# Storing the split weights of the projections in DRAM once and loading the parts again for the later token blocks

## The chip, the cores and the metric

One core of a Trainium2 chip runs the whole kernel. Five engines work side by side, each through its own list of instructions in a fixed order: TensorE (PE, matmuls; its weight loads are shown as PEld), VectorE (DVE), ScalarE (ACT), GpSimd (POOL) and SyncE (SP, which here issues every DMA). An engine waits for another by a semaphore, and what stands behind a waiting instruction in its list waits too. The metric is the time of one execution in microseconds (us) on the device; three runs of the kernel before gave 2217.27, 2220.72 and 2221.74 us, so the median is 2220.72 us.

## The reference, cut to what matters

The input is 2048 tokens of width 1024, float32. One layer is computed.

```python
h = rmsnorm(x, norm_mix)
proj = h @ w_in                      # 1024 x 2832
a_q, a_f, a_i, a_g, b_x, b_g, c_q, c_k, c_v, c_g, c_lr = split(proj)
o_a = hgrn2_mixer(a_q, a_f, a_i, a_g, ...)      # chunked gated linear attention, 4 heads
o_b = rglru_mixer(b_x, b_g, ...)                # causal conv, gates, linear recurrence over tokens
o_c = gla_mixer(c_q, c_k, c_v, c_g, c_lr, ...)  # chunked gated linear attention, 4 heads
x = x + concatenate([o_a, o_b, o_c]) @ w_out    # 1024 x 1024
h = rmsnorm(x, norm_ffn)
gate = causal_dwconv(h @ ffn_w_gate)            # 1024 x 2688
x = x + (gelu(gate) * (h @ ffn_w_val)) @ ffn_w_down
out = rmsnorm(x, norm_final)
```

The change touches only the weights `w_in` and `w_out`.

## The kernel before, in words

**Matmuls in three products.** A float32 operand is split into two parts of type fp32r: the high part is a rounded copy, the low part is what the copy lost (`split`, L110: a copy on one engine, then a subtraction on another). A product is three matmuls, high by high, high by low, low by high (`mm3`, L134).

**Weights.** `load_w` (L115) fetches one piece of a weight matrix, at most 128 partitions by 1024 elements, into a buffer `wr` (pool `wraw`, 3 buffers), and splits it into `wh` and `wl` (pool `wsp`, 3 buffers each). A buffer of `wh`/`wl` is taken again when the matmuls that read it have ended. `W_SPLIT` (L38) says by a tag which engines do the copy and the subtraction, and how far ahead in the priorities the split is put: "z" and "qk" both on DVE, "cv", "ai", "g", "bg" and "out" copy on ACT and subtract on DVE, "bi" copies on DVE and subtracts on POOL.

**Token blocks.** The 2048 tokens are done in four blocks of 512. A block's normed and transposed input `hT` is kept as two parts and, for the first three blocks, stored to DRAM (`h_d`) for a second use.

**First half, groups A and C (L229 to L712).** For every block, `in_steps` projects: two pieces for the forget gates ("z"), three pieces of 272 columns for the values of C ("cv"), four for queries and keys ("qk"), two pieces of 256 columns for the values of A ("ai") and four for the output gates ("g"): 15 calls of `load_w` in a block. `mix_steps` is the chunked attention, many short steps that go from DVE to PE and back. `run_steps` merges the projections of block b+1 with the mixing of block b. In the last block `s_bg` also makes group B's eight projections for that block ("bg") and stores them to DRAM.

**Second half, group B and the output projection (L715 to L875).** `b_in` makes group B's eight projections for the first three blocks ("bi"), reading `hT` again from DRAM, `b_mix` the gates and the recurrence, `b_fin` the split of the concatenated outputs into `oh` and `ol`, and `b_out` the output projection. `b_out` goes through four groups of 256 columns; for each it calls `load_w` twice (rows 0 to 511 and 512 to 1023) and then runs four tiles of 128 tokens, 24 matmuls of 256 columns each, twelve on the first piece and twelve on the second. For every tile a piece of x (`xr`, 4 buffers) is loaded by SP, DVE adds the product to it (L834), and SP stores it to `x2_d`. `b_out` of block b-1 stands behind `b_in` and `b_mix` of block b in the program.

**Third part.** The gated MLP with its own weights, from about 968 us on, until the end.

**Order.** The tile framework lays each engine's list by a priority, which is the place in the program, moved forward where `tc.high_priority` says so, and by when it reckons an instruction can start. `b_in` of block 0 is moved forward to the mixing of the last block. The order on the chip is then fixed.

Of the kernel before, what the change touches and what calls it, by code (L numbers as in the profile page):

```python
# [8 lines left out]
F32 = mybir.dt.float32  # L9
F32R = mybir.dt.float32r  # L10
# [6 lines left out]
P = 128  # L17
D = 1024
KT = D // P
# [14 lines left out]
A_Q, A_F, A_I, A_G, B_X, B_G, C_Q, C_K, C_V, C_G, C_LR = (  # L34
    0, 256, 512, 768, 1024, 1536, 2048, 2176, 2304, 2560, 2816)
# [9 lines left out]
def kernel(ctx: ExitStack, tc: tile.TileContext, x, norm_mix, w_in, hgrn_lower_bounds, hgrn_norm,  # L45
# [4 lines left out]
    vec, act, pool, pe, sync = nc.vector, nc.scalar, nc.gpsimd, nc.tensor, nc.sync  # L50
    x, out, w_in, w_out = x[0], out[0], w_in[0], w_out[0]
# [4 lines left out]
    def pool_at(stack, nbytes, name, bufs, **kw):  # L56

        stack.enter_context(tc.tile_pool(name="pad_" + name, bufs=1, **kw)).tile([P, nbytes // 4], F32, name="pad")
        return stack.enter_context(tc.tile_pool(name=name, bufs=bufs, **kw))
# [3 lines left out]
    wsp = pool_at(ctx, 320, "wsp", 3)  # L63
# [5 lines left out]
    dram = ctx.enter_context(tc.tile_pool(name="dram", bufs=1, space=DRAM))  # L69
# [16 lines left out]
    def mm_bank():  # L86
        return bank("mm", 4)
# [4 lines left out]
    def sc_bank():  # L92
        return bank("sc", 2)
# [10 lines left out]
    def copy(eng, o, i):  # L104
        if eng is act:
            act.activation(o, i, AF.Copy)  # L106
        else:
            eng.tensor_copy(o, i)

    def split(raw, hi, lo, e_hi=act, e_lo=vec):  # L110

        copy(e_hi, hi, raw)
        e_lo.tensor_tensor(lo, raw, hi.bitcast(F32), op=ALU.subtract)  # L113

    def load_w(src, n1, n2, tag, tail=None, wpool=None, wcols=D):  # L115

        def part(pool_, dt, nm):
            return pool_.tile([P, wcols], dt, name=nm, tag=nm)[:, :n1 * n2].rearrange("p (a b) -> p a b", b=n2)
        hl = [part(wpool or wsp, F32R, "wh"), part(wpool or wsp, F32R, "wl")]
        raw = part(wraw, F32, "wr")  # L120
        if tail is None:
            sync.dma_start(out=raw, in_=src)
        else:
            m = src.shape[-1]
            sync.dma_start(out=raw[:, :, :m], in_=src)
            sync.dma_start(out=raw[:, :, m:], in_=tail)
        e_hi, e_lo, ahead = W_SPLIT[tag]
        with tc.high_priority(offset=ahead):
            split(raw, hl[0], hl[1], getattr(nc, e_hi), getattr(nc, e_lo))
        return hl  # L130

    w_in_v = w_in.rearrange("(kt p) c -> p kt c", p=P)
# [46 lines left out]
    def proj_mm(w, hT):  # L179
        o = mm_bank()  # L180
        for kt in range(KT):
            mm3(o, [a[:, kt, :] for a in w], [a[:, kt, :] for a in hT], kt == 0, kt == KT - 1)
        return o

    def proj(hT, col, tag):

        return proj_mm(load_w(w_in_v[:, :, col:col + P], KT, P, tag), hT)

    def merged(a, b):

# [38 lines left out]
    with ExitStack() as cx:  # L229
# [13 lines left out]
        def in_steps(b, B):  # L243
# [13 lines left out]
            def s_vw(col, n):  # L257
                if n > 256:
                    B["V"] = blk.tile([P, NTK, 528], F32, name="V")
                B["kn"] = 3 if n > 256 else 4  # L260
                B["ws"] = []
                for k0 in range(0, KT, B["kn"]):
                    ks = slice(k0, min(k0 + B["kn"], KT))
                    B["ws"].append(load_w(w_in_v[:, ks, col:col + 256], ks.stop - k0, n, "cv" if n > 256 else "ai",
                                          w_in_v[:, ks, C_LR:C_LR + 16] if n > 256 else None))

            def s_v(n, at, t):
                o = mm_bank()
# [42 lines left out]
            for t in range(NTK):  # L311
                steps.append(lambda t=t: (s_vw(C_V, 272) if t == 0 and b > 0 else None, s_v(272, 256, t)))
# [245 lines left out]
        for gi, group in enumerate((rows, frows)):  # L558
            n = sum(r[2] for r in group)
# [7 lines left out]
            cols = const.tile([P, n], F32, name=f"pcol{gi}")  # L567
# [78 lines left out]
        for b in LEVELS[:5]:  # L646
            n = 64 // b
# [67 lines left out]
    with ExitStack() as cy:  # L715
# [3 lines left out]
        with ExitStack() as cx:  # L719
# [12 lines left out]
            w_out_v = w_out.rearrange("(kt p) c -> p kt c", p=P)  # L732
# [87 lines left out]
            def b_out(b, B):  # L820
                oh = B["oh"]
                for qd in range(4):
                    cols = slice(256 * qd, 256 * qd + 256)
                    ws = [load_w(w_out_v[:, k0:k0 + 4, cols], 4, 256, "out") for k0 in (0, 4)]
                    for t in range(NTK):
                        rw = slice(t * P, (t + 1) * P)
                        xr = xrp.tile([P, 256], F32, name="xr")
                        sync.dma_start(out=xr, in_=x[b * TB + t * P:b * TB + (t + 1) * P, cols])
                        o = sc_bank()
                        for kt in range(KT):  # L830
                            mm3(o[:, :256], [a[:, kt, t * P:(t + 1) * P] for a in oh],
                                [a[:, kt % 4, :] for a in ws[kt // 4]], kt == 0, kt == KT - 1)
                        with tc.high_priority(offset=320):
                            vec.tensor_tensor(xr, o[:, :256], xr, op=ALU.add)  # L834
                        sync.dma_start(out=x2_d[b][rw, cols], in_=xr)
# [479 lines left out]
```

## Time and profile before

| what | value |
|---|---|
| median of three runs | 2220.72 us |
| the profiled execution's own time | 2215.95 us |
| its span, first to last instruction | 2214.2 us |
| PE busy | 2142.7 us, 97% |
| DVE busy | 1678.8 us, 76% |
| ACT busy | 987.5 us, 45% |
| POOL busy | 349.3 us, 16% |
| DMA traffic | 321.41 MB, mean 145 GB/s |

A busy PE is not always a PE at its best pace: an instruction's end is modelled, and one that has been issued while the last still drains counts as busy. So the idle time that the profile gives is the least that PE loses. The share of the DMA engines is the mean over the 16 of them. The profile writes an engine's list of issued DMAs as SPq, and a wait of the list on a semaphore is given with whom it waited for.

### The profile page before, as it was taken

What the parts mean: (1) busy time and instruction counts of PE and PEld (TensorE: products, weight loads), DVE (VectorE), ACT (ScalarE), POOL (GpSimd) and SP (SyncE); (2) the same over time, 40 slices, a digit from 0 to 9 for tenths busy, and PEclk for the clock granted to TensorE, in tenths of its full rate; (3) what the DMA queues carried; (4) which work ended last, traced back from release to release, by engine and by line L of the source; (5) the groups of instructions that cost most, each with busy time, mean ns of one, the idle gap of its engine ahead of it and who ended that gap; (6) DMA issues with size and microseconds to landing.
All of it is one profiled execution on the core that took longest, in us unless ns stands there. A gap on an engine that the chain in (4) does not pass through costs nothing.

```text
span 2214.2 us, 31440 instructions
## 1 busy us (share of the span) xinstructions
PE 2142.7 (97%) x12118; PEld 1761.8 (80%) x12118; DVE 1678.8 (76%) x2366; ACT 987.5 (45%) x1361; POOL 349.3 (16%) x456
## 2 busy tenths in 40 slices
PE   7999999999899999999999999999999999999998
PEld 6887778777667878988888887788888887888886
DVE  7799998988768778786676766666666678679676
ACT  3453535433156467454444445544444455226332
POOL 2232341516333231000000000000000000000000
PEclk9999999999999999999999999999999999999999
DMA  7352432345144736643342435522222258667653
GB/s 260 116 180 73 162 97 65 96 148 184 60 136 176 225 121 190 202 136 119 110 134 87 133 95 182 190 80 86 86 86 86 85 176 276 209 205 254 217 174 111
DMA packets 313699, 321.41 MB, mean 145 GB/s; under 512 B 17347, under 2 KB 267214, under 8 KB 312014
## 3 DMA queue, kind: packets, MB, share of 16 engines
q1 hardware_dynamic: 313550, 319.41, 44.5%
q8 instruction: 95, 1.56, 0.3%
q14 instruction: 54, 0.44, 0.1%
HBM read 233.38 MB, written 85.98 MB: 144 GB/s over the span
## 4 chain that ended last, share of the span: by engine, by line
PE 54%; DVE 7%; DMA 5%; ACT 2%; issue 2%; POOL 0%; SPq 0%; DVEq 0%; POOLq 0%; ACTq 0%
PE mm L1072 26%; PE sc L1072 13%; PE aux L1072 6%; PE sc L137 2%; PE sc L138 2%; PE sc L136 2%; DVE wl L113 1%; DMA x_d<-xr 1%; PE mm L138 1%; PE mm L136 1%; PE mm L137 1%; DMA xt<-x_d 1%; DVE xc L801 1%; DMA y<-ps_d 1%; PE mm L913 1%
## 5 line engine op out<-in xcount | busy, mean ns | idle before, releaser
L106 ACT ACTIVATE wh<-wr 128x1024 fp32r<-128x1024 f32 (+3 forms) x217 | 200.8, 928 | 354.6 <-PE mm L1072 91.2
L113 DVE TENSOR_TENSOR wl<-wr,wh 128x1024 fp32r<-128x1024 f32 (+2 forms) x241 | 260.8, 1085 | 102.5 <-ACT wh L106 98.3
L106 ACT ACTIVATE wh<-s 128x1024 fp32r<-128x1024 f32 x116 | 123.0, 1062 | 251.7 <-PE sc L1072 197.8
L138 PE MATMUL mm<-hTh,wl 128*128 128x512 f32 x576 | 231.0, 401 | 2.8 <-POOL wl L113 2.4
L136 PE MATMUL mm<-hTh,wh 128*128 128x512 f32 x576 | 233.6, 406 | 0.0
L137 PE MATMUL mm<-hTl,wh 128*128 128x512 f32 x576 | 231.7, 402 | 0.0
L404 POOL TENSOR_TENSOR qc<-Q,X 32x128 f32<-32x128 f32 x224 | 151.0, 674 | 247.3 <-ACT X L390 116.4
L1072 PE MATMUL mm<-t34h,wh 128*128 128x512 f32 x464 | 181.1, 390 | 1.3 <-DVE y L1238 0.9
L1072 PE MATMUL mm<-t34h,wl 128*128 128x512 f32 x464 | 180.6, 389 | 0.0
L1072 PE MATMUL mm<-t34l,wh 128*128 128x512 f32 x464 | 180.5, 389 | 0.0
L113 DVE TENSOR_TENSOR wl<-s,wh 128x1024 fp32r<-128x1024 f32 x116 | 141.4, 1221 | 18.5 <-ACT wh L106 18.4
L137 PE MATMUL sc<-wl,oh 128*128 128x256 f32 x512 | 146.8, 287 | 2.4 <-DVE wl L113 2.4
L136 PE MATMUL sc<-wh,oh 128*128 128x256 f32 x512 | 146.3, 287 | 0.2 <-DVE xr L834 0.2
L138 PE MATMUL sc<-wh,ol 128*128 128x256 f32 x512 | 145.4, 284 | 0.0
L138 PEld LDWEIGHTS mm<-hTh,wl 128*128 128x128 f32 x576 | 108.6, 189 | 31.1 <-issue 4.3
L136 PEld LDWEIGHTS mm<-hTh,wh 128*128 128x128 f32 x576 | 108.4, 188 | 28.9 <-issue 6.8
L137 PEld LDWEIGHTS mm<-hTl,wh 128*128 128x128 f32 x576 | 108.7, 189 | 27.8 <-issue 7.3
L1141 DVE SCALAR_TENSOR_TENSOR ga<-gr,pcol,ga 128x1024 f32<-128x1024 f32 x84 | 107.6, 1281 | 0.4 <-issue 0.3
L1072 PEld LDWEIGHTS mm<-t34h,wh 128*128 128x128 f32 x464 | 87.1, 188 | 21.2 <-issue 1.7
L137 PEld LDWEIGHTS sc<-wl,oh 128*128 128x128 f32 x512 | 97.5, 190 | 5.8 <-DVE wl L113 3.0
L1072 PEld LDWEIGHTS mm<-t34h,wl 128*128 128x128 f32 x464 | 87.1, 188 | 18.2
L1072 PEld LDWEIGHTS mm<-t34l,wh 128*128 128x128 f32 x464 | 87.1, 188 | 17.9
(335 smaller groups left out, 5508.4 us busy)
## 6 DMA issues: line engine op xcount, KB each, us to landing
wr<-in_w_in_dram SPq DMA_DIRECT2D x80, 512.0 KB
wr<-in_ffn_w_gate_dram SPq DMA_DIRECT2D x42, 512.0 KB
wr<-in_ffn_w_val_dram SPq DMA_DIRECT2D x42, 512.0 KB
wr<-in_w_out_dram SPq DMA_DIRECT2D x32, 512.0 KB
gr_d<-v SPq DMA_DIRECT2D x32, 512.0 KB
ps_d<-y SPq DMA_DIRECT2D x32, 512.0 KB
wr<-gr_d SPq DMA_DIRECT2D x32, 512.0 KB
wr<-in_ffn_w_down_dram SPq DMA_DIRECT2D x25, 512.0 KB
```

Of the source, the lines that this page charges most:

```text
L106: act.activation(o, i, AF.Copy)
L113: e_lo.tensor_tensor(lo, raw, hi.bitcast(F32), op=ALU.subtract)
L136: pe.matmul(o, lh, rh, start=first, stop=False)
L137: pe.matmul(o, lh, rl, start=False, stop=False)
L138: pe.matmul(o, ll, rh, start=False, stop=last)
L404: pool.tensor_tensor(qc[p_, h, :].rearrange("p (n s) -> p n s", s=lev), qo[p_, 2], xo[p_, 2], op=ALU.mult)
L801: vec.tensor_tensor_scan(xc[:, i, :], r[:, i, :], th[:, i, :], initial=hs0[:, c:c + 1], op0=ALU.mult, op1=ALU.add)
L913: pe.transpose(out=pt[:, k * P:(k + 1) * P], in_=xt[:, (k0 + k) * P:(k0 + k + 1) * P], identity=ident)
L1072: pe.matmul(o, lhs[a], rhs[b], start=first and k == 0 and i == 0, stop=last and k == KH - 1 and i == 2, skip_group_check=True)
L1141: vec.scalar_tensor_tensor(ga, gr[:, k:k + TH], pc[f"fw{k}"][:, f:f + 1], ga, op0=ALU.mult, op1=ALU.add)
```

## The change

A dictionary `parts_d` holds, for each key, two DRAM tensors. `load_w` takes a key. The first call with a key loads and splits as before, and then stores both parts to DRAM, two DMAs from SP. Every later call with that key takes buffers of `wh` and `wl` and loads the two parts straight into them, two DMAs in place of one, with no split. Keys are given by the projections of `in_steps` and `b_in` (the column), by the values' pieces, and by `b_out`. Group B's keys are first met in `s_bg`, in the last block of the first half, so there it is that block that stores and the three others that load.

```diff
+    parts_d = {}
+
-    def load_w(src, n1, n2, tag, tail=None, wpool=None, wcols=D):
+    def load_w(src, n1, n2, tag, tail=None, key=None):
 
         def part(pool_, dt, nm):
-            return pool_.tile([P, wcols], dt, name=nm, tag=nm)[:, :n1 * n2].rearrange("p (a b) -> p a b", b=n2)
-        hl = [part(wpool or wsp, F32R, "wh"), part(wpool or wsp, F32R, "wl")]
+            return pool_.tile([P, D], dt, name=nm, tag=nm)[:, :n1 * n2].rearrange("p (a b) -> p a b", b=n2)
+        hl = [part(wsp, F32R, "wh"), part(wsp, F32R, "wl")]
+        if key in parts_d:
+            for a, d in zip(hl, parts_d[key]):
+                sync.dma_start(out=a.bitcast(F32), in_=d)
+            return hl
         raw = part(wraw, F32, "wr")
...
             split(raw, hl[0], hl[1], getattr(nc, e_hi), getattr(nc, e_lo))
+        if key is not None:
+            parts_d[key] = [dram.tile([P, n1, n2], F32, name=f"w_{tag}{len(parts_d)}_{i}") for i in range(2)]
+            for a, d in zip(hl, parts_d[key]):
+                sync.dma_start(out=d, in_=a.bitcast(F32))
         return hl
...
-        return proj_mm(load_w(w_in_v[:, :, col:col + P], KT, P, tag), hT)
+        return proj_mm(load_w(w_in_v[:, :, col:col + P], KT, P, tag, key=col), hT)
...
-                                          w_in_v[:, ks, C_LR:C_LR + 16] if n > 256 else None))
+                                          w_in_v[:, ks, C_LR:C_LR + 16] if n > 256 else None, key=("v", col, k0)))
...
-                    ws = [load_w(w_out_v[:, k0:k0 + 4, cols], 4, 256, "out") for k0 in (0, 4)]
+                    ws = [load_w(w_out_v[:, k0:k0 + 4, cols], 4, 256, "out", key=("o", qd, k0)) for k0 in (0, 4)]
```

The calls of `load_w` for `ffn_w_down` give no key and are as before.

## Rows read from the trace of the kernel before

**Rows 1.** Busy time by stretch: PE, PEld, DVE, ACT, POOL, clock, DMA share, GB/s.

```profile
core 0: us, PE busy (x) PEld busy (x) DVE busy (x) ACT busy (x) POOL busy (x), PEclk, DMA share, GB/s
0.00:112.00 112.00, 96.83 (x576) 81.48 (x577) 80.73 (x175) 48.03 (x75) 26.78 (x48) 1.00 0.58 190
112.00:545.00 433.00, 418.41 (x3507) 336.07 (x3507) 394.38 (x660) 181.87 (x280) 144.85 (x205) 1.00 0.38 121
545.00:582.00 37.00, 31.11 (x303) 23.35 (x302) 35.58 (x57) 8.96 (x17) 18.25 (x26) 1.00 0.39 129
...
650.00:702.00 52.00, 45.23 (x183) 34.30 (x182) 50.64 (x48) 34.92 (x42) 26.19 (x17) 0.95 0.32 102
702.00:751.00 49.00, 48.77 (x386) 47.10 (x385) 30.80 (x38) 22.86 (x25) 6.56 (x4) 0.98 0.87 294
...
803.00:860.00 57.00, 54.89 (x411) 48.84 (x410) 42.73 (x56) 41.07 (x45) 7.04 (x11) 1.00 0.58 183
860.00:915.00 55.00, 54.00 (x415) 50.38 (x414) 40.53 (x50) 32.81 (x39) 4.94 (x5) 1.00 0.51 162
...
885.00:910.00 25.00, 25.00 (x211) 25.00 (x210) 16.73 (x21) 9.94 (x10) 2.19 (x2) 1.00 0.58 185
968.00:2214.20 1246.20, 1230.01 (x5425) 1012.34 (x5423) 874.06 (x1108) 539.72 (x732) 67.47 (x108) 1.00 0.44 143
```

**Rows 2.** Waits of PE, 112 to 968 us: total us, times, longest us.

```profile
PE sc L427 <- DVE qa L400: 9.4, 8, 2.8
PE aux L775 <- ACT r L777: 6.0, 2, 4.6
...
PE sc L137 <- DVE wl L113: 2.4, 3, 1.0
PE mm L138 <- POOL wl L113: 2.4, 1, 2.4
PE mm L137 <- DVE wl L113: 1.5, 1, 1.5
```

**Rows 3.** Weight splits by form, 112 to 968 us: busy us, mean ns, idle before.

```profile
L113 DVE TENSOR_TENSOR wl<-wr,wh 128x1024 fp32r<-128x1024 f32 x75 | 92.4, 1240 | 9.5 <-ACT wh L106 9.0
L113 POOL TENSOR_TENSOR wl<-wr,wh 128x1024 fp32r<-128x1024 f32 x24 | 63.8, 2659 | 107.0 <-DVE wh L108 46.2 <-DMA oa<-o_ac_d 19.9 <-PE mm L138 18.4
L106 ACT ACTIVATE wh<-wr 128x1024 fp32r<-128x1024 f32 x59 | 61.5, 1051 | 49.3 <-PE sc L138 26.7 <-PE mm L137 18.2 <-PE mm L138 4.1
L108 DVE CAST wh<-wr 128x1024 fp32r<-128x1024 f32 x40 | 30.2, 756 | 13.3 <-PE mm L137 12.0 <-PE mm L138 1.1
```

**Rows 4.** DMA issues of the two weights: count, KB each.

```profile
wr<-in_w_in_dram SPq DMA_DIRECT2D x80, 512.0 KB
...
wr<-in_w_out_dram SPq DMA_DIRECT2D x32, 512.0 KB
```

**Rows 5.** One DVE instruction beside POOL's subtraction, timeline: start us, us.

```profile
667.04 3.26 POOL L113 TENSOR_TENSOR wl<-wr,wh 128x1024 fp32r<-128x1024 f32 x1 [2.66 <-DVE wh L108]
```

**Rows 6.** The same stretch on DVE, timeline.

```profile
667.96 3.43 DVE L792 SCALAR_TENSOR_TENSOR xc<-gi,xc 128x1024 f32<-128x1024 f32 x1
```

**Rows 7.** The chain that ended last, 640 to 970 us: start us, us, what.

```profile
717.96 3.13 DMA xr<-in_x_dram
...
736.72 4.82 DMA x_d<-xr
...
763.11 1.23 DVE xc L792
...
931.00 4.24 DMA xt<-x_d
```

**Rows 8.** A split in `b_out` of block 2, timeline of ACT.

```profile
888.82 1.06 ACT L106 ACTIVATE wh<-wr 128x1024 fp32r<-128x1024 f32 x1 [1.41 <-PE sc L138]
```

**Rows 9.** The same split's second half, timeline of DVE.

```profile
889.91 1.23 DVE L113 TENSOR_TENSOR wl<-wr,wh 128x1024 fp32r<-128x1024 f32 x1
```

**Rows 10.** Waits of SP's list, 800 to 968 us: total us, times, longest us.

```profile
SPq L828 <- DMA x_d<-xr: 48.0, 33, 3.6
```

## The prediction

> **What bounds the kernel now.** I read the busy time by stretch first, then PE's waits, then the splits by form, and last the chain and SP's own waits where the change puts new DMAs. The change ends at 968 us: what follows (1246 us, PE busy 1230) uses other weights [rows 1], so only the first 968 us count. There PE is close to full: 418.41 of 433 us in the mixing of the later blocks, 48.77 of 49, 54.89 of 57 and 54.00 of 55 us in the output projections [rows 1]. No matmul is removed, so what can be won is PE's idle time, and only that. Two stretches are DVE's: 545 to 582 us, with DVE at 35.58 of 37 and PE idle 5.9, and 650 to 702 us, with DVE at 50.64 of 52 and PE idle 6.8. From 112 to 545 us DVE is at 91% and PE idle 14.6 [rows 1]. PE's waits on a weight's split are small: 2.4, 2.4 and 1.5 us [rows 2].
>
> **What the change removes.** Calls with a key: 15 in each of four blocks, 8 in `s_bg`, 24 in `b_in`, 32 in `b_out`. First calls: 15, 8 and 8. So 45 + 24 + 24 = 93 splits go: on DVE 42 copies of 0.756 us (31.8 us), 36 + 24 full subtractions of 1.240 us (74.4 us) and nine smaller ones, at three quarters of that or less (8 us); on ACT 42 full copies of 1.051 us and nine smaller ones (51 us); on POOL all 24 subtractions of 2.659 us (63.8 us) [rows 3].
>
> *Term a, waits on a split that go.* 2.4 + 2.4 + 1.5 = -6.3 us [rows 2]; at worst none goes.
>
> *Term b, a freer DVE.* From 112 to 545 us, 18 copies, 36 subtractions and the small ones leave DVE, some 66 of its 394 us. PE's waits that name DVE's work for the mixing are 9.4 us for `qa` [rows 2]; I take 4.5 of the 14.6 us of idle. In the two stretches where DVE is the bound, each projection frees 0.756 us and what POOL takes from DVE besides: L792 took 3.43 us beside a POOL subtraction that ran 3.26 us, and 1.23 us without one [rows 5 to 7], 2.2 us more. Four or five projections in each stretch make about 12 us, which is more than the idle; what is late next is the chain through ACT (PE waited 6.0 us for `r`) [rows 2]. I take 8.5 of 12.7 us. Sum -13 us; bounds 0 and -27.3, the whole idle of the three.
>
> The Trainium skill, SBUF — State Buffer, "Who interferes with whom", says that a VectorE instruction with two SBUF inputs and a GpSimd instruction that reads SBUF exclude each other for the whole length of the one that came first. By that rule the 3.43 us are a lock and 24 times 2.2 us, an estimate of 53 us, come back to DVE; the trace agrees in the one place cited.
>
> **What it adds.** 62 stores and 93 more loads. A full piece is 512 KB [rows 4]; the parts of one block's 15 keys are 12 times two of 512 KB and three smaller pairs (816, 816 and 544 elements a partition), 14.8 MB; `s_bg`'s and `b_out`'s are 8.4 MB each. All are issued by SP, in its order.
>
> *Term c, the output projections of blocks 1 to 3.* A buffer is now filled by DMA after PE has let it go, where a piece waiting in `wr` was split into it. Three buffers, two in use: of a group's two pieces one comes early, the other takes the buffer that the first piece of the group before leaves twelve matmuls before that group's end, and is read twelve matmuls into the next. With 25.00 us for 211 matmuls [rows 1], 0.118 us each, that leaves 24 of them, 2.84 us, for the high part and one more for the low, 2.96. Now: PE lets go at 888.82, the low part is there at 889.91 + 1.23 = 891.14, after 2.3 us: hidden [rows 8, 9]. Then: a 512 KB load took 4.24 us from issue to landing [rows 7], the second part's bytes at 294/0.87 = 338 GB/s [rows 1] another 1.55, so 4.24 to 5.8 us; I take 5.5. If the planner puts the first half of the next tile in between (two PSUM buffers allow it), 1.42 us more are covered: 1.1 us late. SP is also held: 33 waits of 1.45 us for a store to land before an `xr` load [rows 10], and a weight load stands behind one about half the time: 0.7. That is 1.8 us for a group, for the eight groups of blocks 2 and 3 +14.4 us; the four of block 1 I count at nothing, because `b_mix`'s matmuls stand between them; if these are gone from there, they cost another 7. Bounds: 0 (all hidden) and 12 times (5.8 - 2.96 + 1.45) = 51 us. Queued behind such a wait are the `xr` loads and stores, and for these DVE and then PE's banks wait.
>
> The Trainium skill, DMA: Bandwidth & Descriptors, "Anatomy of one DMA", gives for one DMA issued from GpSimd 2.0 us and the bytes at 436 GB/s. By that rule both parts would be there after an estimated 4.4 us, just what is covered with the half tile, and c would be SP's waits alone, +6; the row of 4.24 us for the first part speaks against it.
>
> *Term d, the stores in the output projection of block 0.* From 702 to 751 us the DMA engines are at 0.87, 42.6 us of work in 49, with PE full [rows 1]; 8.4 MB more are 24.8 us: 67.4 us of work in 49. The store and the load of `xr` are already on the chain there, 4.82 and 3.13 us [rows 7], and each would stand behind parts in the queue. Some of the excess of 18.4 us goes over into the stretch behind, some stops PE: +8; bounds 0 and 18.4.
>
> *Term e, the stores in the first block.* Up to 112 us the share is 0.58, 65 us of work; 14.8 MB at 190/0.58 = 328 GB/s are 45 more, 110 of 112. The loads that PE needs next stand behind stores: +4; bounds 0 and as much as PE idles there now, 15.2. `s_bg`'s 8.4 MB, 25 us of work, fall where the share is 0.38 on the mean and I count them at nothing; half of that if they meet the reload of `hT`.
>
> *Term f, the third values' piece.* It takes the buffer of the second "z" projection and is read 18 matmuls later, 2.3 us by the pace above, with 4.24 us at most to land and mixing steps in between: +1 in each of three blocks, +3; bounds 0 and 9. The other projections have a buffer free two projections ahead, two times 24 matmuls of double width, 11 us: the load is hidden. SP's own issuing is no bound.
>
> **Sum.** -6.3 - 13 + 14.4 + 8 + 4 + 3 = +10.1 us on the profiled execution's 2215.95, 2226. The median of the runs is 4.8 us above that execution, so I expect a median of 2231 us.
>
> **Rivals.** *Faster.* The loads come in time (c, d, e and f at 5 together) and DVE's relief goes through to PE, most of the 27 us of term b and all of a: 5 - 6.3 - 21 = -22, 2199 us. For it: DVE at 91 to 97% in three stretches, and POOL's subtractions gone. Against: most of PE's idle is spread over chains from engine to engine, which a freer DVE does not shorten.
>
> *Nothing moves.* Loads are hidden, and PE's lists have room for few gains: a and b at a third, c to f at a third, +3; within 4 us of before, 2221 us. For it: PE is full in most stretches. Against: the tight buffer of term c is there in every group.
>
> *A convoy at SP, slower by much.* One list issues everything in order. A load that waits for PE to let a buffer go holds the `xr` loads behind it, late `xr` holds DVE's additions, these hold the two PSUM banks, and PE lets go later still. It decides once a group's chain, now store 4.82 + load 3.13 + SP's wait 1.45 = 9.4 us [rows 7, 10] for four tiles of 24 matmuls, 11.3 us, grows by over 1.9. Then c is near its bound and d with it: 42 + 15 + 7 - 15 = +49 us before what is hidden; I price it at +40, 2261 us.
>
> That the parts are not reused at all is no case: in program order every key is met first by the call that stores, and `b_in`'s columns are `s_bg`'s.
>
> **How the numbers follow.** The forecast 0.44 (own range 2217 to 2246; 0.13 of it falls within 0.2%, 0.31 above), faster 0.33, nothing 0.10 (0.02 faster, 0.06 same, 0.02 slower), convoy 0.13. A measurement can tell about 0.2%, 4.4 us, from no change. Faster 0.35, same 0.19, slower 0.46. The range takes in the middle of the faster case and of the convoy: 2198 to 2263.
>
> **What would show it.** Term a and b: no POOL subtraction before 968 us, DVE under 80% from 112 to 545 us, PE idle from 650 to 702 us under 4. Term c: PE's waits for a DMA into `wh` or `wl` at L137 and L136 of some 14 us from 860 to 968 us. Term d: a DMA share near 1 around the first output projection and PE idle there. Wrong if PE shows no waits on those loads, if 860 to 968 us stay 108 us long, or if the planner puts PE's work in another order and the stretch from 545 to 650 us moves by more than the terms here.

## The result, and the profile after

The changed kernel took 2240.07 us (median of 6 runs, 2234.65 to 2243.79); the kernel before took 2220.64 us beside it (6 runs, 2217.27 to 2228.41). The ratio is 1.0082, 95% interval [1.006, 1.0104]: slower by 19.4 us in the medians. The two profiled executions lie further apart, 2242.89 against 2215.95 us, and what follows explains these 26.9 us stage by stage; the one is near the slow end of its kernel's runs and the other below those timed, so the sizes below are good to a few us, not better.

The page of the kernel after, busy time by engine, and the DMA line:

```profile
PE 2153.8 (96%) x12118; PEld 1771.7 (79%) x12118; DVE 1544.5 (69%) x2255; ACT 940.7 (42%) x1308; POOL 264.4 (12%) x432
...
DMA packets 270980, 400.40 MB, mean 179 GB/s; under 512 B 16611, under 2 KB 192750, under 8 KB 269294
```

DVE lost 134 us of work, POOL 85 and ACT 47; the DMA engines moved 79 MB more. PE has the same 12118 matmuls. Its busy time is 11 us longer, and it stands idle longer too. The stretches that answer to [rows 1], in the kernel after (the same columns; the work inside is shifted by up to 25 us):

```profile
0.00:112.00 112.00, 86.27 (x445) 72.46 (x446) 64.65 (x149) 37.52 (x55) 16.39 (x34) 0.94 0.78 277
112.00:545.00 433.00, 421.20 (x3504) 338.62 (x3503) 336.91 (x601) 165.09 (x265) 131.09 (x203) 1.00 0.54 192
545.00:582.00 37.00, 35.47 (x301) 27.25 (x299) 29.58 (x54) 9.14 (x19) 17.19 (x30) 1.00 0.92 326
...
650.00:702.00 52.00, 49.93 (x207) 38.22 (x206) 42.25 (x48) 38.65 (x45) 9.48 (x11) 1.00 0.67 241
702.00:751.00 49.00, 42.60 (x296) 37.21 (x295) 30.86 (x35) 31.73 (x36) 2.69 (x5) 0.97 0.81 301
```

Read them against [rows 1]. In the first 112 us PE ran 445 matmuls where it had run 576, and its clock was granted at 0.94: this is the largest loss. From 650 to 702 us PE's idle time fell from 6.8 to 2.1 us with DVE at 42.25 in place of 50.64: the gain that was forecast. From 702 to 751 us PE fell from 48.77 to 42.60; there the output projection of block 0 now stores its parts.

To place the difference I took the time of the same matmul in both traces. "First mixing step" is the first matmul of L359 (L370 after) of a block, "mixing ends" the last of L516 (L527), `out` the output projection's matmuls. The changes are taken before rounding.

| mark | before, us | after | change | between two marks |
|---|---|---|---|---|
| first mixing step, block 0 | 79.5 | 98.2 | +18.7 | +18.7 |
| first mixing step, block 3 | 485.8 | 503.6 | +17.7 | -1.0 |
| mixing ends, block 2 | 544.5 | 560.8 | +16.3 | -1.4 |
| mixing ends, block 3 | 636.5 | 642.3 | +5.8 | -10.5 |
| `out` of block 0, first | 693.8 | 702.4 | +8.7 | +2.9 |
| `out` of block 0, last | 750.7 | 765.4 | +14.7 | +6.0 |
| `out` of block 1, first | 804.3 | 811.1 | +6.8 | -7.9 |
| `out` of block 1, last | 858.2 | 869.3 | +11.1 | +4.3 |
| `out` of block 2, last | 913.3 | 926.1 | +12.8 | +1.7 |
| `out` of block 3, last | 968.9 | 994.0 | +25.1 | +12.3 |
| end of the trace | 2214.2 | 2241.2 | +27.0 | +1.9 |

So there are gains of some 21 us (mixing of the last blocks, the projections between the first two output projections) and losses of some 48: 18.7 in the start-up, 6.0 in the storing output projection, 18.3 in the loading ones, and 4.8 in two other places.

**Where the start-up lost its time.** SP's list in the kernel before, from its timeline (start us, us, line, what it issued):

```profile
5.69 0.49 SPq L126 DMA_DIRECT2D wr<-in_w_in_dram  x1
6.35 2.21 SPq L151 DMA_DIRECT2D xt<-in_x_dram  x2
...
16.88 2.04 SPq L122 DMA_DIRECT2D wr<-in_w_in_dram  x3
```

The same list in the kernel after:

```profile
5.85 0.47 SPq L133 DMA_DIRECT2D wr<-in_w_in_dram  x1
10.12 0.34 SPq L140 DMA_DIRECT2D w_cv<-wh  x1
...
15.26 0.32 SPq L140 DMA_DIRECT2D w_cv<-wl  x1
15.62 1.11 SPq L162 DMA_DIRECT2D xt<-in_x_dram  x2
...
24.58 0.42 SPq L129 DMA_DIRECT2D wr<-in_w_in_dram  x1
35.86 0.34 SPq L238 DMA_DIRECT2D h_d<-hTh  x1
36.59 0.33 SPq L238 DMA_DIRECT2D h_d<-hTl  x1
39.31 0.32 SPq L140 DMA_DIRECT2D w_z<-wh  x1
40.57 0.36 SPq L140 DMA_DIRECT2D w_z<-wl  x1
40.98 9.54 SPq L129 DMA_DIRECT2D wr<-in_w_in_dram  x3
```

Six stores of the "cv" parts stand in the list where the third and fourth input tile stood. Each waits for the split that writes what it stores, so the list stands still: the tiles are called for at 15.62 us in place of 6.35, the next weight at 24.58 in place of 16.88, and the one after it, behind two stores of `h_d` and two of "z", at 40.98. In the kernel before three weights had gone out by 18.9 us. PE pays at the other end (timeline of PE, kernel after; in brackets the idle time before and who ended it):

```profile
48.70 1.12 PE L295 MATMUL aux<-lr,gup 16*128 16x512 f32 x2 [1.22 <-DVE lr L293]
55.72 0.79 PE L147 MATMUL mm<-hTh,wh 128*128 128x512 f32 x1 [5.90 <-DVE wh L108]
...
57.58 0.63 PE L147 MATMUL mm<-hTh,wh 128*128 128x512 f32 x1
58.00 0.63 PE L148 MATMUL mm<-hTl,wh 128*128 128x512 f32 x1
...
59.70 0.39 PE L149 MATMUL mm<-hTh,wl 128*128 128x512 f32 x1
59.92 0.40 PE L147 MATMUL mm<-hTh,wh 128*128 128x512 f32 x1
```

`DVE wh L108` is the copy of the weight that was called for late. By windows of 20 us, kernel after:

```profile
20.00:40.00 20.00, 15.26 (x90) 14.07 (x90) 10.26 (x22) 5.26 (x10) 2.27 (x7) 0.83 0.32 119
40.00:60.00 20.00, 12.04 (x43) 7.82 (x43) 15.74 (x61) 5.75 (x8) 0.00 (x0) 0.83 0.91 335
60.00:80.00 20.00, 20.00 (x90) 16.53 (x89) 10.64 (x15) 7.90 (x10) 0.55 (x1) 1.00 0.97 348
```

and the first two of them, kernel before:

```profile
20.00:40.00 20.00, 18.64 (x119) 16.16 (x118) 16.18 (x62) 5.24 (x9) 2.36 (x7) 1.00 0.69 259
40.00:60.00 20.00, 20.00 (x89) 15.59 (x88) 14.95 (x30) 9.66 (x11) 0.00 (x0) 1.00 0.80 267
```

Between 20 and 40 us the DMA engines are *less* busy than before (0.32 against 0.69), because the list that feeds them waits; then they have it all at once (0.91 and 0.97). That is a queue's signature, not yet proof of it.

The loss has two parts. Up to the first mixing step, kernel before and then kernel after:

```profile
0.00:79.50 79.50, 66.06 (x381) 56.88 (x381) 56.45 (x142) 35.75 (x52) 17.36 (x34) 1.00 0.62 207
0.00:98.20 98.20, 72.47 (x383) 61.40 (x386) 58.13 (x141) 35.02 (x51) 16.39 (x34) 0.93 0.78 277
```

PE is idle for 25.7 us in place of 13.4, and busy 6.4 us longer with the same work, at a granted clock of 0.93, a mean of the levels 1.2 and 2.4 GHz, in place of 1.00. So 12.3 of the 18.7 us are idle time, and 6.4 go with the lower clock (an estimate from the clock alone: 0.07 of 98.2 us, 6.9).

**Where the loading output projections lost theirs.** PE's waits from 112 to 968 us, kernel after (total us, times, longest):

```profile
PE sc L147 <- DMA wh<-w_out: 6.7, 6, 1.9
...
PE sc L438 <- DVE qa L411: 2.3, 5, 0.8
```

The first line is new: PE waits for a part of `w_out` to land. To the end of the last output projection (994 us) it is 9.1 us in 7 waits. Two such loads in the chain that ended last, start and length to landing (the six in it up to 994 us took 4.27 to 6.00 us):

```profile
839.82 4.63 DMA wh<-w_out
...
854.85 6.00 DMA wh<-w_out
```

The second line shows the gain: waits for the mixing's `qa` were 9.4 us [rows 2].

### The profile page after: what moved, and what is told of

The parts are those of the page before. It is cut to its first block, busy times and chain, and to the rows that moved or that the text cites. A ratio compares the mean times of both kernels' runs of the same rounds, so it can differ in the third digit from the quotient of the medians.

```text
span 2241.2 us, 31400 instructions
## 1 busy us (share of the span) xinstructions
PE 2153.8 (96%) x12118; PEld 1771.7 (79%) x12118; DVE 1544.5 (69%) x2255; ACT 940.7 (42%) x1308; POOL 264.4 (12%) x432
## 4 chain that ended last, share of the span: by engine, by line
PE 77%; DVE 9%; DMA 6%; ACT 3%; issue 2%; POOL 1%; SPq 0%; DVEq 0%; POOLq 0%; ACTq 0%
PE mm L1083 26%; PE sc L1083 13%; PE mm L147 7%; PE mm L149 7%; PE mm L148 6%; PE aux L1083 6%; PE sc L147 2%; PE sc L149 1%; PE sc L148 1%; PE sc L438 1%; DMA wh<-w_out 1%; DVE wl L113 1%; DMA y<-ps_d 1%; PE sc L487 1%; DVE qa L411 1%
## 5 line engine op out<-in xcount | busy, mean ns | idle before, releaser
L106 ACT ACTIVATE wh<-wr 128x1024 fp32r<-128x1024 f32 (+2 forms) x166 | 150.3, 906 | 319.3 <-PE mm L1083 99.5
L113 DVE TENSOR_TENSOR wl<-wr,wh 128x1024 fp32r<-128x1024 f32 (+2 forms) x172 | 178.4, 1039 | 99.3 <-ACT wh L106 95.1
L415 POOL TENSOR_TENSOR qc<-Q,X 32x128 f32<-32x128 f32 x224 | 142.6, 637 | 272.9 <-ACT X L401 117.4
L113 DVE TENSOR_TENSOR wl<-s,wh 128x1024 fp32r<-128x1024 f32 x116 | 141.6, 1222 | 20.1 <-ACT wh L106 20.0
L147 PEld LDWEIGHTS sc<-wh,oh 128*128 128x128 f32 x512 | 98.9, 194 | 20.5 <-DMA wh<-w_out 11.9
```

The lines of the kernel that those rows point to most:

```text
L147: pe.matmul(o, lh, rh, start=first, stop=False)
L415: pool.tensor_tensor(qc[p_, h, :].rearrange("p (n s) -> p n s", s=lev), qo[p_, 2], xo[p_, 2], op=ALU.mult)
```

## Experiments

**Theories.** *List order*: stores cost because they wait in SP's list for a split with urgent loads behind them. Rival: *bandwidth*, the stores cost by their bytes. For the output projections, *late buffer*: a loaded part has no raw buffer to land in early, so its load starts when PE lets go of the last group. Rivals: SP's list, or the bytes. And for the gain: *DVE and POOL relieved*, all of which should be in group B's weights.

All runs, each against the kernel before on the same chip (2217.5 to 2218.7 us):

| what keeps its parts | median us | ratio [95%] |
|---|---|---|
| groups A and C (`e1`) | 2232.71 | 1.0081 [1.005, 1.0111] |
| group B, "bg" and "bi" (`e2`) | 2200.65 | 0.9924 [0.9899, 0.9949] |
| output projections (`e3`) | 2236.18 | 1.0092 [1.0068, 1.0116] |
| all, input tiles issued first (`e4`) | 2234.45 | 1.0082 [1.0055, 1.0108] |
| A and C: a small part of each store, no loads (`e5`) | 2229.45 | 1.005 [1.0033, 1.0067] |
| all, stores in ACT's list (`e6`) | 2238.7 | 1.0083 [1.0068, 1.0098] |
| out, first piece of a group (`e7`) | 2228.77 | 1.0035 [1.0023, 1.0048] |
| out, second piece of a group (`e8`) | 2245.34 | 1.0119 [1.0102, 1.0136] |
| A and C, from block 1 on (`e9`) | 2215.1 | 0.9985 [0.9965, 1.0004] |
| out, second piece loaded into raw buffers (`e10`) | 2243.37 | 1.0109 [1.0084, 1.0134] |
| B, and A and C from block 1 on (`e11`) | 2196.75 | 0.9901 [0.9879, 0.9923] |
| out, no load behind the last group (`e12`) | 2231.91 | 1.0062 [1.0034, 1.0089] |

Their marks, as changes in us against the trace of the kernel before:

| mark | e1 | e2 | e3 | e4 | e5 | e6 | e7 | e8 | e9 | e10 | e11 | e12 |
|---|---|---|---|---|---|---|---|---|---|---|---|---|
| first mixing step, block 0 | +18.8 | +1.3 | +1.2 | +20.4 | +10.6 | +12.0 | -0.1 | +0.3 | +1.3 | +0.1 | +0.1 | +0.1 |
| mixing ends, block 2 | +17.8 | +0.1 | +1.8 | +20.7 | +12.9 | +11.3 | +0.3 | +0.5 | -0.7 | +0.2 | -3.7 | +0.3 |
| mixing ends, block 3 | +17.8 | -9.0 | +1.8 | +10.2 | +19.3 | +0.7 | +1.1 | +1.3 | +6.4 | +1.1 | -12.8 | +1.1 |
| `out` 0, first | +17.8 | -3.9 | +1.8 | +12.3 | +19.3 | +3.8 | +1.1 | +1.1 | +6.3 | +1.1 | -8.3 | +1.1 |
| `out` 0, last | +18.8 | -10.8 | +9.5 | +19.0 | +18.9 | +7.0 | +5.3 | +6.3 | +7.1 | +6.9 | -15.2 | +10.6 |
| `out` 1, first | +18.7 | -13.6 | +8.4 | +11.2 | +19.5 | +9.0 | +4.0 | -0.2 | +7.4 | +6.1 | -15.7 | +8.6 |
| `out` 1, last | +18.9 | -13.4 | +15.3 | +14.5 | +19.5 | +13.0 | +5.8 | +16.9 | +7.7 | +9.0 | -15.1 | +10.2 |
| `out` 2, last | +18.9 | -13.4 | +17.7 | +15.9 | +19.5 | +16.6 | +9.4 | +22.6 | +7.6 | +15.5 | -15.1 | +10.7 |
| `out` 3, last | +21.1 | -8.3 | +23.7 | +23.8 | +21.1 | +22.2 | +14.7 | +30.5 | +8.3 | +20.9 | -12.0 | +17.8 |

`e2`, `e3` and `e9` store nothing before the first mixing step of block 0. Their +1.2 and +1.3 us there go with a granted clock of 0.91 from 20 to 40 us, where the kernel before and `e11` have 1.00.

**The three parts alone.** `e1`, groups A and C only:

```diff
-        return proj_mm(load_w(..., tag, key=col), hT)
+        return proj_mm(load_w(..., tag, key=None if tag in ("bg", "bi") else col), hT)
-  ws = [load_w(..., "out", key=("o", qd, k0)) for k0 in (0, 4)]
+  ws = [load_w(..., "out") for k0 in (0, 4)]
```

> Keys for the projections of groups A and C alone (block 0 stores 15 pieces, blocks 1 to 3 load them). Theory, three places: the changed kernel loses 18.7 us up to the first mixing step of block 0 and gives 2.4 back by the end of block 2's mixing, so this part alone should stand at +14 to +18 us to the kernel before, all of it there by the first mixing step at about 98 us (79.5 before). Rival, the whole 79 MB of extra traffic slows everything a little: a third to a half of it is here, so +8 to +12, spread over 0 to 545 us.

`e2`, the opposite in the first line (`key=col if tag in ("bg", "bi") else None`), no key for the values' pieces and none for "out":

> Keys for group B's projections alone (the last block of the first half stores 8 pieces, b_in of the three others loads 24). Theory, three places: this is where the change wins, 10.5 us in the mixing of the last block and 8 us in block 2's projections, with some 3 lost between; alone -8 to -16 us to the kernel before. Rival, traffic: +5 to +8. Rival, the planner's order by chance: within 4 us of the kernel before.

`e3`, only "out" keeps its key:

> Keys for the output projection's weights alone. Theory, three places: 6 us in the output projection of block 0 (stores), 6 in blocks 1 and 2 and 12 in block 3 and what follows it (loads that wait for a buffer): +15 to +25 us to the kernel before, nothing changed up to 650 us, and PE waits for DMA into wh of about 9 us. Rival, the losses there come from lateness in group B's part and not from these loads: within 5 us of the kernel before.

The three add up to +14.3 - 17.7 + 17.8 = +14.4 us in the medians, near the +19.4 of the whole. `e1` has all its loss at the first mixing step, +18.8 us, the same as the whole change: group B's and the output's stores have no part in it. What stays for it of DVE's relief is 1.0 us up to the end of the mixing (+18.8 to +17.8). `e2` is a gain by itself, 1.7 us more than the most that was expected. (Its trace is of an execution at 2207.77 us, 7 above the median, so its marks show less of it.) By the marks 9.1 us lie in the last block's mixing, 5.1 are lost again before the first output projection, 6.9 lie from the first to the last matmul of that projection, and 2.8 between it and the next. The stretch that answers to the one from 650 to 702 us in [rows 1], in `e2`:

```profile
650.00:702.00 52.00, 48.52 (x235) 39.20 (x234) 39.96 (x47) 38.86 (x47) 9.70 (x11) 1.00 0.64 236
```

POOL's 26.19 us of work there are 9.70, DVE's 50.64 are 39.96, and PE ran 235 matmuls in place of 183. `e3` loses 7.7 us in block 0, which only stores, and 6.9, 2.4 and 6.0 us in the blocks that load.

**Start-up: order or bytes.** `e4` calls for the input tiles ahead of the first weights:

```diff
-        blocks[0]["load"]()
         for f in nx.load[2:]:
             f()
+        blocks[0]["load"]()
```

> The changed kernel with the loads of block 0's third and fourth tile of x put ahead of the first weights in the program, so that they no longer stand behind the first stores in SP's list. Theory, order in SP's list: the first mixing step comes at 84 to 90 us instead of 98.2 and the time falls by 8 to 14 us against the changed kernel, to 2226 to 2232 us. Rival, bandwidth of the stores in block 0: the same stores take the same DMA time, the first mixing step stays at 95 us or later and the time within 4 us of the changed kernel.

That expectation fell: the first mixing step came at 99.9 us, where the rival had asked for 95 or later. PE's waits up to there name another load (`pstage`, the small constants):

```profile
PE aux L577 <- DMA pstage<-in_ffn_conv_w_dram: 10.2, 1, 10.2
```

The tiles came in time, and the stores stopped what stood behind them next. So it is not this one load; whatever follows in the list is late.

`e5` keeps the waits and the order of the list but stores only the first of the rows of each A and C piece (2.7 MB of 14.8), and loads nothing back:

```diff
-        if key in parts_d:
-            ...
-        if key is not None:
+        if key is not None and key not in parts_d:
...
-                sync.dma_start(out=d, in_=a.bitcast(F32))
+                sync.dma_start(out=d[:, :1, :], in_=a[:, :1, :].bitcast(F32))
```

> Block 0 stores of each piece of groups A and C only the first of its 2 to 8 row groups (2.6 MB in place of 14.8), and nothing is loaded back: every block splits as the kernel before. What is stored is read by nobody. Theory, order in SP's list: the same stores wait for the same splits in the same list, so the first mixing step still comes at 92 to 99 us (79.5 before) and the time is +12 to +18 us to the kernel before. Rival, bandwidth: with a sixth of the bytes the first mixing step comes at 80 to 84 us and the time is within 4 us of the kernel before.

The first mixing step came at 90.1 us, between the theory's 92 to 99 and the rival's 80 to 84. With under a fifth of the bytes, 10.6 of the 18.7 us are still lost, and the wait for the late weight is there unshortened (PE's waits up to 95 us):

```profile
PE mm L143 <- DVE wh L108: 6.2, 2, 5.9
```

The other 8 us went with the bytes. So both count: the wait in the list, with the 2.7 MB that are left, for 10.6 us, and the rest of the bytes for 8.

`e5` also lost 6.4 us in the last block's mixing. Its trace has the lower clock there, as that of `e9` has:

```profile
582.00:640.00 58.00, 55.88 (x338) 35.52 (x338) 31.58 (x55) 8.07 (x12) 12.07 (x11) 0.88 0.14 37
```

The kernel before has 1.00 in this stretch; the line stands with `e9`.

`e6` moves the stores to ACT's list, so that SP's is as before:

```diff
-                sync.dma_start(out=d, in_=a.bitcast(F32))
+                act.dma_start(out=d, in_=a.bitcast(F32))
```

> The changed kernel with all its stores of parts issued from ACT's list in place of SP's; the same bytes move. Theory, order in SP's list: the loads of x, of the small constants and of the weights go out as in the kernel before, the first mixing step comes at 80 to 88 us and 8 to 18 us are won against the changed kernel, less what ACT loses by waiting for DVE's subtraction; 2222 to 2232 us. Rival, bandwidth: first mixing step still at 95 us or later, the time within 5 us of the changed kernel.

The first mixing step is at +12.0 us (91.5), later than the theory asked for and earlier than the rival. Now ACT's own work stands behind the stores' waits (ACT's longest wait up to 100 us):

```profile
ACT hTh L106 <- DVE wl L113: 9.3, 1, 9.3
```

`hTh` is an input that PE needs next, `wl L113` the split that a store waits for. PE's own waits up to 95 us name splits of weights, `DVE wl L113` with 4.3 and `DVE wh L108` with 2.4 us, and `hTh` with 0.2 only; how ACT's wait reaches PE is argued, not shown. At the end nothing is won, 1.0083: the time is within 5 us of the changed kernel, as the rival had it, so `e6` does not tell the list from the bytes.

`e9` lets groups A and C store in block 1 and load in blocks 2 and 3 (block 0 splits and stores nothing; group B and "out" split as before):

```diff
+    late_d = []
...
+        return proj_mm(load_w(..., key=None if tag in ("bg", "bi") or not late_d else col), hT)
...
+                late_d.append(b)
```

> The input projections of groups A and C are kept from block 1 on: block 1 stores its parts, blocks 2 and 3 load them; block 0, the conv branch and the output projections split as before. Theory (block 0's loss is that six stores, each waiting for a split, stand in SP's list ahead of loads that the start-up needs at once, with all the input still to come): stores placed in a block whose weights were called for long before take nothing, so the first mixing step of block 0 stands at 79.5 us within 0.5, block 3's at 485.8 within 3, and the whole lies between -3 and +2 us of before. Rival (the stores cost by their bytes wherever they stand): the same 8.4 MB in block 1 delay block 1's mixing by about what half of the +18.7 of block 0 was, so block 3 starts its mixing at 493 to 497 us and the whole is at +7 to +12 us.

(The 8.4 MB in that text are a slip; block 1 stores the 14.8 MB that block 0 stored.) The same stores, issued between 93 and 198 us, cost nothing: block 1 starts its mixing at 233.2 us, as in `e2` (233.2) and `e3` (233.1), which store nothing there, and block 3 at 485.1 us (before: 485.8), where the rival asked for 493 to 497. (Block 0's first step, at 80.8, is outside the 0.5 us that were allowed, by the clock named above.) The stores of groups A and C cost in the start-up, and there alone. The trace is of an execution at 2224.95 us, where the median is 2215.1: 7.1 of its 9.0 us come up in the last block's mixing, where it shows

```profile
582.00:640.00 58.00, 56.13 (x238) 33.48 (x237) 28.00 (x48) 10.64 (x15) 13.89 (x11) 0.85 0.18 50
```

238 matmuls at a clock of 0.85. The kernel before has, in the same stretch,

```profile
582.00:640.00 58.00, 56.12 (x273) 35.24 (x273) 32.13 (x55) 14.12 (x19) 14.91 (x11) 1.00 0.28 84
```

The ten runs of `e9` together are at 0.9985 [0.9965, 1.0004].

**Output projections: the late buffer.** A group of `b_out` takes two pieces. `e7` keeps only the first (`key=("o", qd, k0) if k0 == 0 else None`), `e8` only the second (`k0 == 4`):

> Keys for the output projection alone, and there only for each group's first piece, whose buffer comes free a whole group ahead; the second piece is split as before. Theory, the late buffer: no wait for a DMA into wh in blocks 1 to 3 (under 3 us in all, 13.4 with both pieces), half of the loss of the stores in block 0: 0 to +6 us to the kernel before, +18 with both. Rival, the loads cost by their number and traffic whichever buffer they take: half of the loss, +8 to +10, and as much for the second pieces.

> Keys for the output projection alone, and there only for each group's second piece, whose buffer comes free twelve matmuls before the group ends. Theory, the late buffer: waits of PE for a DMA into wh of 9 us or more, about what it has with both pieces, and +10 to +16 us to the kernel before. Rival, number and traffic: +8 to +10, the same as for the first pieces alone.

PE's waits on loads of `w_out` are 13.4 us in `e3`, none in `e7`, and in `e8`, from 690 to 1002 us:

```profile
PE aux L786 <- ACT r L788: 14.2, 2, 9.5
PE sc L147 <- DMA wh<-w_out: 11.6, 9, 2.4
```

So the waits belong to the second piece, as the theory says. But neither time came out as expected: `e7` is at +10 where 0 to +6 was expected, and `e8` at +26.6, worse than both pieces together. The +10 is what the rival, number and traffic, had asked for, so late buffers explain the waits on loads and not the whole loss. From 690 to 1000 us `e7` has in their place

```profile
PE sc L147 <- DVE xr L845: 5.0, 7, 1.4
```

PE waits for DVE's addition of x, which holds the bank that the next tile is to take; from 690 to 970 us the kernel before has 0.2 us of it. In `e8` the first line adds 9 us that are not the load's (in `e3` the same wait is 4.7 us): a gate activation that the conv branch's matmuls waited for. What made it late was not settled.

`e10` is `e3` with the second piece's two parts loaded into the three raw buffers, which idle in the loading blocks:

```diff
+        own = key in parts_d and key[2] == 4
+        hl = [part(wraw, F32R, "wr") for _ in range(2)] if own else [part(wsp, F32R, "wh"), part(wsp, F32R, "wl")]
```

> Only the output projections keep their parts, as in the run with these alone (2236.2 us, +17.8), and the second piece's two parts are loaded into the three raw buffers, which the loading blocks otherwise leave idle, so the loads of a group need not wait for the matmuls of the group before it. Theory (late buffer: in that run the loads were called for only when the last matmul of the group before had freed the buffer, 9 waits of 13.4 us): the waits of PE on loads of w_out fall to 0 to 4 us; the stores of block 0 (+7.7 by the end of its output projection) stay; blocks 1 to 3 add 0 to +2 each in place of +7, +2.7, +6; the whole at +5 to +11 us. Rival (the loads are late by their number and bytes, 1 MB a piece in place of 0.5 MB, not by the buffer): waits of 10 us or more stay, whole at +14 to +20 us.

The waits stayed; they moved to the tile that now holds the part (758 to 992 us):

```profile
PE sc L149 <- DMA wr<-w_out: 12.1, 9, 2.0
```

The layout was at fault: with three buffers for two parts a group, every group's low part takes the buffer of the high part of the group before, which PE holds to its last matmul. One late load of four costs as much as two, and the time, +25.9 us, is above what either case had. `e12` mends that: with six small-part buffers and three raw ones no part takes a buffer of the group just before.

```diff
+        hl = [part(wraw, F32R, "wr") if own else part(wsp, F32R, "wh"),
+              part(wraw, F32R, "wr") if own and key[1] % 2 == 0 else part(wsp, F32R, "wl")]
```

> Only the output projections keep their parts, and the second piece's parts are laid into the idle raw buffers and one buffer of the small parts in such a turn that no load of a group waits for the matmuls of the group just before it (in the run before this one, one load of four still did, and PE's waits stayed at 12.1 us). Theory (late buffer): PE's waits on loads of w_out fall to 0 to 4 us, blocks 1 to 3 add 0 to +3 us in all after the stores' +7 in block 0, and the whole is at +5 to +11 us. Rival (the loads are late by SP's list or by their bytes): waits of 8 us or more stay. Third (the waits go, and the loss stays): the time goes elsewhere in the output projections, +14 to +20 us with waits under 4.

PE's longest waits from 762 to 988 us, `e12`:

```profile
PE mm L926 <- DVE xt L170: 7.6, 3, 3.7
PE mm L149 <- DVE wh L108: 2.9, 1, 2.9
PE sc L149 <- DVE xr L847: 2.5, 1, 2.5
```

No wait on `w_out` is among PE's waits any more, and blocks 1 and 2 take +1.6 and +0.5 us where `e3` took +6.9 and +2.4. That settles the late buffer for these two. The whole, 1.0062, is not far enough from `e3`'s 1.0092 for the intervals to part; the stages tell them apart. Its +13.4 us lie above the theory's +5 to +11 and just under the third case's +14 to +20: the waits went, a good part of the loss stayed. What stays is block 0, +9.5 us, and block 3, +7.1 us, where the first line stands: the first transposes of the MLP, which PE runs between the last output projection's matmuls, waited 3.2 us in all before and 7.6 now. `e7`, without any late load, loses 5.3 us there too, and `e2` loses 5.1, though its output projections are as before. Block 3's output projection, kernel before and then `e2`:

```profile
913.10:968.90 55.80, 51.97 (x445) 51.14 (x444) 50.35 (x82) 33.33 (x54) 3.23 (x6) 1.00 0.61 199
899.90:960.60 60.70, 54.06 (x443) 53.59 (x443) 50.47 (x82) 33.45 (x54) 3.23 (x6) 0.94 0.56 182
```

So a loss of this size in block 3 comes without any stored part of `w_out`, with a granted clock of 0.94 in place of 1.00 and 2.8 us more of idle time. What sets it off was not settled.

**The version that beats both.** `e11` has `e2`'s keys from the start and `e9`'s from block 1 on (`key=col if tag in ("bg", "bi") or late_d else None`):

> Two parts of the change together: group B's projections keep their parts as in the run with these alone (ratio 0.9924 to before), and groups A and C keep theirs from block 1 on (0.9985 alone); the output projections and the conv branch of block 0 split as before. Theory (the gain is VectorE and GpSimd freed in the last block's mixing and block 2's projections; stores at start-up cost, stores later do not): the two add up, ratio 0.989 to 0.993, the first mixing step of block 0 at 79 to 81 us, the last block's mixing 9 us or more shorter than before. Rival (the loads of both take the DMA engines and SP's list from each other in block 3): the second undoes part of the first, ratio 0.995 to 1.002.

2196.75 us (2192.77 to 2202.08), 0.9901 of the kernel before [0.9879, 0.9923]; by the medians that is 22 us below the kernel before and 43 below the changed one. The first mixing step is where it was, and the last block's mixing is 9.1 us shorter. Its intervals touch `e2`'s, so that late keys for A and C add to `e2` is likely by the marks (-3.7 us at the end of block 2's mixing, +0.1 in `e2`, where 1.3 are the clock's at the start), not proved by the times.

## Why the prediction came out as it did

The direction and the mechanism of the largest gain and of the largest term of the sum held, and the forecast median, 2231 us, is near the 2240 measured. The size of the change did not hold: +10.1 us was forecast, +19.4 came by the medians and +27.0 between the traces. One term was far off, and no row that it was worked out from shows SP's list in the start-up.

**Term e, +4 forecast, +18.7 measured.** This is the mis-sized one. It was worked out as bandwidth, 110 us of transfers in 112 us, with the list as an afterthought; "the loads that PE needs next stand behind stores" was there, and priced at 4 us. What was priced at next to nothing is the store's *wait*: each of the first six stands in SP's list until its split is done. `e5` still loses 10.6 us with 2.7 of the 14.8 MB, `e9` puts the whole loss on the start-up, and 6.4 of the 18.7 us go with the lower clock, which the sum did not have. The term's upper bound, 15.2 us, was what PE idled there before, and a bound from existing idle says nothing about new idle.

**Terms a and b, -19.3 forecast.** The marks between which they fall add to -1.0 - 1.4 - 10.5 + 2.9 - 7.9 = -17.9 us in the whole change, and `e2` alone gave -17.7 in the medians. All signs that were named appeared: DVE at 336.91 of 433 us (78%), PE idle 2.1 us from 650 to 702, and no subtraction of a split on POOL. Inside it the split was off: of the 4.5 us from 112 to 545 us about 1 came, and the last block's mixing gave more than its stretch from 545 to 582 us had of idle (5.9 us). Between its marks, kernel before and then kernel after:

```profile
544.50:636.50 92.00, 84.23 (x563) 56.33 (x562) 66.83 (x111) 19.61 (x33) 33.58 (x37) 1.00 0.30 92
560.80:642.30 81.50, 78.08 (x552) 53.32 (x551) 52.01 (x104) 19.53 (x32) 14.39 (x30) 1.00 0.42 150
```

Idle time fell from 7.8 to 3.4 us, 4.4 of the 10.5; the rest is 6.2 us less of busy time with 11 matmuls fewer. Twelve more stand between the next two marks (238 for 226), so part of the -10.5 is work that went behind the mark, and it belongs with the +2.9 there: -7.6 us together.

DVE's work fell by 134.3 us in the whole change, of which the splits that went are 114 by their rows. `e2` shows by itself what came back with POOL's subtractions; from its page:

```profile
PE 2138.8 (97%) x12118; PEld 1764.5 (80%) x12118; DVE 1625.3 (74%) x2342; ACT 988.0 (45%) x1361; POOL 276.2 (13%) x432
```

DVE lost 53.5 us there (1678.8 before), of which 24 copies of 0.756 us are 18.1; 35.4 us more came back. The Trainium skill, SBUF — State Buffer, "Who interferes with whom", by whose lock an estimated 53 us more were to come back to DVE, agrees in kind and not in size: these 35 us did.

**Term c, +14.4 forecast for blocks 2 and 3, 0 for block 1.** Measured +4.3, +1.7 and +12.3 in the whole change; +6.9, +2.4 and +6.0 in `e3`, the waits 13.4 us there and 9.1 in the whole. The mechanism is right (`e7`, `e8`, `e12`), the landing of 4.27 to 6.00 us lies about where it was put (4.24 to 5.8), and the sum is near, in part by luck: block 1 was not covered by `b_mix`, block 2 was better covered than thought, and block 3's is only in part this term, as `e2` loses 5.1 us there without it. Of the 14 us of waits that were named as the sign, 6.6 came (869 to 994 us). That late additions of x would hold PE's banks was named and not priced; `e7` has 5.0 us of it. The Trainium skill, DMA: Bandwidth & Descriptors, "Anatomy of one DMA", gave an estimated 4.4 us for both parts, from its figures for a DMA issued from GpSimd; the 4.27 to 6.00 us of single parts issued from SP here speak against it for this case.

**Term d, +8 forecast:** +6.0 in the whole, +7.7 in `e3`. The size came, the reason was not seen: it was worked out from full DMA engines, with a share near 1 as the sign, and the share from 702 to 751 us is 0.81, where it was 0.87 before. What the trace shows is the list again, SP's waits from 695 to 762 us in the kernel after:

```profile
SPq L140 <- ACT wh L106: 8.3, 5, 3.6
SPq L140 <- DVE wl L113: 6.6, 5, 3.2
```

SP stood for 14.9 us before stores whose split was not done. No run takes this wait away and keeps the bytes, so which of the two costs PE its 6 us stays open.

**Term f, +3 forecast:** nothing. From block 0's first mixing step to block 3's the kernel got 1.0 us faster, `e1` 0.9.

**Rivals.** The faster case did not come for the whole change; its price, 2199 us, is what group B alone gives (2200.65). The convoy at SP did not come as written. In the start-up the one list does hold loads up, at near half of the convoy's price, but behind stores that wait for splits; a load waits for PE there once, for 0.9 us, and no `xr` is involved. In the output projections SP's waits for `xr` stores to land, 48.0 us from 800 to 968 us [rows 10], are the same in the kernel after, from 811 to 994 us:

```profile
SPq L839 <- DMA x_d<-xr: 48.1, 25, 3.4
```

## What to carry to other kernels

A store of a value that is still being computed blocks, in an in-order list of issues, every load behind it: put such stores where the loads behind them are not yet wanted (here one block later, at no cost), or leave them out at the start. To trade computing for traffic pays where the engine relieved sets the end and the load has a buffer free ahead of its use; ask both for each group of weights by itself, since here one group gave 18 us and the two others took 32. A buffer that is refilled by DMA must come free a whole landing (here 4.27 to 6.00 us) earlier than one that is refilled from a neighbouring buffer.

## What the runs showed of the hardware

After PE had stood idle for 5.90 us (and 1.22 us shortly before), its 512-column matmuls started 0.42 us apart from 57.58 to 59.28 us and 0.22 us apart from 59.70 us on; the granted clock of that window of 20 us is 0.83, a mean of the levels 1.2 and 2.4 GHz. The eight steps from 55.72 to 59.70 us took 3.98 us, at 0.22 us each they take 1.76: the lower clock behind the wait cost PE some 2.2 us more. The same clock shows from 20 to 40 us, where PE was busy for 15.26 of 20 us.

With loads and stores of 512 KB queued, the DMA engines moved 326, 335 and 348 GB/s at shares of 0.92, 0.91 and 0.97, so 354 to 368 at a full share, where the stretches of [rows 1] give 316 to 338.
